# Retention values in products of 512 columns, second and last queries added behind their decayed keys, and the gated unit's operands loaded by halves

## The chip, the core and the metric

The kernel runs on one core of a Trainium2 chip. Its time is the device time of one execution in microseconds (us); where several runs are shown, the median counts. The profile is one execution of its own, whose instructions were recorded.

## What is computed

A trunk of two layers on an input x of 1024 tokens by 1024 channels, all in float32. Cut to what matters here:

```python
h = rmsnorm(x, norm_g[0])
u_s5, g_s5, q, k, v, g_ret = split(h @ w_in)          # 1024 x 1024 each, q and k 1024 x 512
# branch A: a diagonal complex state-space layer, then a gated linear unit
y = gelu(s5(u_s5));  y_s5 = y * sigmoid(y @ glu_w + glu_b) * silu(g_s5)
# branch B: retention, 8 heads, keys of 64 and values of 128, chunks of 64 tokens
q, k = rope(q) / 8, rope(k)                            # rotary positions
scores = q @ k.T * intra_decay                         # inside a chunk
kv = (k * k_decay).T @ v;  s = chunk_decay * s + kv    # state from chunk to chunk
y_ret = headnorm(scores @ v + (q * q_decay) @ s) * silu(g_ret)
x = x + concat(y_s5, y_ret) @ w_out
# layer 1: a gated causal convolution of 31 taps with its own normalisation, then a final rmsnorm
```

The output must agree with float32, so each projection is done as three products of rounded halves: `wh*xh + wh*xl + wl*xh`, where `h` is the rounded high part (type fp32r) and `l` is what is left.

## The kernel before

All activations lie transposed: 128 channels on the partitions, tokens along the free dimension, in two halves of 512 tokens. One tensor engine (PE) does the products; its instruction stream is written in program order and rearranged by a scheduler that looks at expected times, and every engine then works through its own list in order. So does SP, which issues nearly all DMAs: an issue that waits holds up all issues behind it.

**Weights.** `plan` writes down the order in which 512 KB weight blocks are used, `wnext` takes the next one and issues the loads of the two behind it, and `wload` loads a block (tile `wf`, three buffers), copies the high part on ACT (`wh`, line 133, three buffers) and subtracts for the low part on POOL (`wl`, line 134, three buffers). So the high part of a block can be made only once PE is through with the block three places before it, and its load only once POOL is through with that one.

**Retention** (`retention`, line 784 on) goes over four pairs of heads. For a pair, `ret_proj` projects keys and queries (`mm_k`, `mm_q`: 48 products of 512 columns each, the weights stationary), turns them by their positions, and then projects the values. Turning (`turn`) needs a copy of the raw tile with swapped 32-row blocks (`swp`, one buffer, four DMAs on SP, line 831), four products with the tables on POOL (lines 834 and 835) and two additions on DVE (line 836). The values (`mm_v`, lines 859 to 861) have the tokens as the stationary operand, and 256 columns of weights (one pair of heads) as the moving one: per pair 8 blocks of 128 tokens, each 24 products of 256 columns, collected in the three banks of `ps_mm` and scaled by ACT (line 862).

`ret_heads` then transposes the keys (`ktp`), multiplies them by the decay on DVE (`kt`, line 876), and does the small products `kv`, `sp`, `ro` and `rt`, with DVE work between them (states `S`, masked scores `sc`, normalisation). The scheduler puts the projections of the next pair between them, and after the last pair the products of the gated unit (`mm_glu`). I call this stretch, from the first `ktp` to the last `rt`, a **seam**.

`y_pass` reads the state-space result (`yp`), applies gelu on ACT (`yn`, line 781) and stores it; two of the eight go with each pair, and from the second pair on they wait for the last root of the pair before.

**The gated unit.** `load_split(self.yn_d, "y", False)` loads the eight operand blocks of 128 channels with all 1024 tokens each (`yf`, line 997, in the buffers of `wf`), and splits each half on ACT (`yh`, line 968) and DVE (`yl`, line 969). The split tiles take the place of the layer's first operands (`xh`, `xl`, still read by `mm_v`): those of the first half are free when the fourth token block of the last pair's values is done, those of the second when the eighth is.

The table of convolution taps (`convw`) is halved on DVE in line 1102 after its DMA. In `h1` the eight blocks `x1n` of the first half share five buffers with other tiles.

Of the kernel before, what the change touches and what calls it, by code (L numbers as in the profile page):

```python
# [11 lines left out]
F32 = mybir.dt.float32  # L12
# [27 lines left out]
class Trunk:  # L40
# [734 lines left out]
    def y_pass(self, rp, cb):  # L775

        nc = self.nc
        yt = rp.tile([P, 8, P], F32, name=f"yp_{cb}", tag="yp", bufs=1)
        nc.sync.dma_start(yt[:], self.y_d[cb].rearrange("i h g m -> (h g) i m"))
        yn = rp.tile([P, P, 8], F32, name=f"yn_{cb}", tag="ynt", bufs=2)  # L780
        nc.scalar.activation(yn[:], yt[:].rearrange("p i m -> p m i"), AF.Gelu_apprx_tanh)
        nc.sync.dma_start(self.yn_d[cb * P:(cb + 1) * P], yn[:].rearrange("p m i -> p (m i)"))

    def retention(self, st):
# [10 lines left out]
        self.g128 = rp.tile([P, 4], F32, name="g128")  # L795
        nc.sync.dma_start(self.g128[:], A["ret_g128"])
        for pair in range(4):
            cur = self.ret_proj(pair)
            with ExitStack() as held:
                if pair:  # L800
                    held.enter_context(self.tc.issue_after(self.last_rs.ins))
                for cb in (2 * pair, 2 * pair + 1):
                    self.y_pass(rq, cb)
            if pair == 3:
                early.close()
                self.lp = self.pool("l1", side="right")
            self.ret_heads(pair, *cur)

    def ret_proj(self, pair):
# [40 lines left out]
        vt = rp.tile([P, 8, 256], F32, name=f"v_{pair}", tag="v", bufs=2)  # L850
        for b in range(8):
# [10 lines left out]
            nc.scalar.mul(vt[:, b, :], ps[:, :256], self.Rtok[:, b:b + 1])  # L862
        return krot, qrot, vt

    def ret_heads(self, pair, K, Q, V):
        nc, rp = self.nc, self.rp
# [3 lines left out]
        for hf in range(2):  # L870
            ps = self.bank(f"ktp{hf}_{pair}")
            for b in range(4):
                t0 = (4 * hf + b) * P
                nc.tensor.transpose(ps[:, b * P:(b + 1) * P], K[:, t0:t0 + P], self.ident[:])
            kd = self.kdec[:, 2 * pair:2 * pair + 2, :].rearrange("p h d -> p (h d)")
            v.tensor_tensor(kt[:, 4 * hf:4 * hf + 4, :], ps[:].rearrange("p (b d) -> p b d", b=4),
                            kd.unsqueeze(1).broadcast_to([P, 4, P]), op=ALU.mult)

        S = rp.tile([P, 8, P], F32, name=f"S_{pair}", tag="S", bufs=1)
        for hf in range(2):  # L880
            ps = self.bank(f"kv{hf}_{pair}")
            for b4 in range(4):
# [3 lines left out]
                for hh in range(2):  # L886
                    r = slice(64 * hh, 64 * hh + 64)
                    nc.tensor.matmul(ps[r, b4 * P:(b4 + 1) * P], kt[:, b, r], V[:, b, hh * P:(hh + 1) * P],
                                     start=True, stop=True)
# [31 lines left out]
        for hf in range(2):  # L921
            pss = [self.bank(f"ro{hf}_{2 * pair + hh}") for hh in range(2)]

            def products():
# [7 lines left out]
                for hh in range(2):  # L932
                    for b4 in range(4):
                        b = 4 * hf + b4
                        yield nc.tensor.matmul(pss[hh][:, b4 * P:(b4 + 1) * P], sc[hh][:, b, :],
                                               V[:, b, hh * P:(hh + 1) * P], start=False, stop=b4 == 3)
            last_ro = self.chained(products())
# [28 lines left out]

    def split(self, src, hi, lo, eng):
        self.nc.scalar.copy(hi[:], src)  # L968
        eng.tensor_tensor(lo[:], src, hi[:].bitcast(F32), op=ALU.subtract)  # L969

    def layer0_back_and_layer1(self, st):
# [9 lines left out]
        def load_split(src, name, halves):  # L981
            res = [[], []]

            def put(kb, h, f):
                a, b = (self.op_tile(self.opA, f"A{h}", f"{name}{q}{kb}_{h}") for q in "hl")
                self.split(f, a, b, v)
                res[h].append((a, b))
            if halves:
                for h in range(2):
                    for kb in range(KB):  # L990
                        f = lp.tile([P, HALF], F32, name=f"{name}f{kb}_{h}", tag="tp", bufs=3)
                        nc.sync.dma_start(f[:], src[rows(kb), hs(h)])
                        put(kb, h, f[:])
            else:
                for kb in range(KB):
                    f = self.wp.tile([P, T], F32, name=f"{name}f{kb}", tag="wf", bufs=3)
                    nc.sync.dma_start(f[:], src[rows(kb)])
                    for h in range(2):
                        put(kb, h, f[:, hs(h)])
            return res  # L1000
# [8 lines left out]
        for nb, h in [(nb, h) for nb in range(6) for h in range(2)] + [(6, 0), (7, 0), (6, 1), (7, 1)]:  # L1009
# [13 lines left out]
            nc.scalar.mul(a[:], sg[:], 0.5)  # L1023
            v.scalar_tensor_tensor(b[:], sg[:], 0.5, a[:].bitcast(F32), op0=ALU.mult, op1=ALU.subtract)
            ys[h][nb] = (a, b)
# [22 lines left out]
        def h1(h):  # L1048
# [3 lines left out]
            for kb in range(KB):  # L1052
                t = (opB.tile([P, HALF], F32, name=f"x1n{kb}_{h}", tag="B1") if h else
                     lp.tile([P, HALF], F32, name=f"x1n{kb}_{h}", tag="u", bufs=5))
                nc.sync.dma_start(t[:], self.x1_d[rows(kb), hs(h)])
# [45 lines left out]
        nc.sync.dma_start(cw[:], A["conv_w"])  # L1101
        v.tensor_scalar(cw[:], cw[:], 0.5, None, op0=ALU.mult)
        cv = [[None] * 8 for _ in range(2)]
# [274 lines left out]
def layout(inp):  # L1378
# [61 lines left out]
```

## Time and profile before

| | |
|---|---|
| median of 3 runs | 1219.36 us (1218.27 to 1221.7) |
| the profiled execution, its own time | 1219.24 us |
| its span, from first to last instruction | 1217.5 us |
| granted clock of PE over the span | 0.997 |
| PE busy, DVE, POOL, ACT | 1199.5, 747.1, 653.9, 480.6 us |

What the execution takes outside the span is 1219.24 - 1217.5 = 1.7 us. In the rows of the profile, a group of instructions stands with its source line, engine and operation, what it writes and reads by tile name, the shapes, the count behind an x, and its busy time and mean duration. A row of the windows view gives the length of a stretch and, for each engine, its busy time and in brackets how many instructions touched it. In the timeline, square brackets give the idle time before an instruction and what ended it.

### The profile page before, as it was taken

Reading aid. Unit: us, or ns where it says so; the run is one execution under the profiler, and the core shown is the slowest. Engines: PE = TensorE matmul, PEld = TensorE weight load, DVE = VectorE, ACT = ScalarE, POOL = GpSimd, SP = SyncE. Lnnn points to the kernel's source line nnn. Section 1 sums busy time; section 2 is a strip of 40 time slices with the busy share of each in tenths; the row PEclk is TensorE's granted clock in tenths of the full one; section 3 lists DMA queues with packets and bytes.
Section 4 is the critical chain, followed back from the end, with each engine's and each line's share of the span. In section 5 each row is a group of like instructions: output and inputs, shape, how many; then the busy total and the mean of one; then the engine's idle time right before and its main releaser. Section 6 shows DMA issues by size and latency. Waiting matters only on the chain.

```text
span 1217.5 us, 17581 instructions
## 1 busy us (share of the span) xinstructions
PE 1199.5 (99%) x6660; PEld 1011.3 (83%) x6660; DVE 747.1 (61%) x1337; ACT 480.6 (39%) x712; POOL 653.9 (54%) x453
## 2 busy tenths in 40 slices
PE   9999999999999999998999999999999999999997
PEld 7888888888889999997888888788888888888876
DVE  7965555555413635546746101599999799999533
ACT  7212233322222323134434322545545575434652
POOL 2059988888124333342454551578453467758642
PEclk9999999999999999999999999999999999999998
DMA  8342433333384536266446776755677654356764
GB/s 333 104 139 74 152 128 124 133 131 124 107 268 139 176 102 195 82 216 220 165 156 216 269 270 254 260 188 196 222 253 251 232 182 155 123 176 236 243 250 147
DMA packets 98500, 225.03 MB, mean 185 GB/s; under 512 B 9072, under 2 KB 38000, under 8 KB 97776
## 3 DMA queue, kind: packets, MB, share of 16 engines
q1 hardware_dynamic: 98416, 223.92, 54.9%
q8 instruction: 52, 0.85, 0.3%
q14 instruction: 32, 0.26, 0.1%
HBM read 158.41 MB, written 61.28 MB: 180 GB/s over the span
## 4 chain that ended last, share of the span: by engine, by line
PE 91%; DMA 4%; DVE 2%; ACT 1%; POOL 1%; issue 1%; SPq 1%; DVEq 0%; POOLq 0%
PE mm_g L143 7%; PE mm_g L144 7%; PE mm_g L142 7%; PE mm_wo L144 5%; PE mm_wo L142 5%; PE mm_wo L143 5%; PE mm_a L144 2%; PE mm_b L144 2%; PE mm_a L143 2%; PE mm_a L142 2%; PE mm_b L143 2%; PE mm_u L144 2%; PE mm_u L143 2%; PE mm_b L142 2%; PE mm_u L142 2%; PE mm_glu L144 2%
## 5 line engine op out<-in xcount | busy, mean ns | idle before, releaser
L1142 DVE SCALAR_TENSOR_TENSOR cv<-u,convw,cv 128x512 f32<-128x512 f32 x398 | 273.4, 751 | 11.9 <-ACT cv L1128 9.6
L1122 POOL TENSOR_TENSOR tp<-tp,tp 128x512 f32<-128x512 f32 x64 | 83.1, 1298 | 44.4 <-ACT tp L1121 43.3
L144 PE MATMUL mm_g<-xh,wl_g 128*128 128x512 f32 x256 | 100.8, 394 | 0.0
L143 PE MATMUL mm_g<-xl,wh_g 128*128 128x512 f32 x256 | 100.6, 393 | 0.0
L142 PE MATMUL mm_g<-xh,wh_g 128*128 128x512 f32 x256 | 100.5, 393 | 0.0
L861 PE MATMUL mm_v<-wh_v,xl 128*128 128x256 f32 x256 | 72.5, 283 | 0.0
L860 PE MATMUL mm_v<-wl_v,xh 128*128 128x256 f32 x256 | 72.4, 283 | 0.0
L859 PE MATMUL mm_v<-wh_v,xh 128*128 128x256 f32 x256 | 72.4, 283 | 0.0
L134 POOL TENSOR_TENSOR wl_v<-wf_v,wh_v 128x1024 fp32r<-128x1024 f32 x8 | 19.2, 2396 | 88.6 <-ACT wh_v L133 88.6
L1121 ACT ACTIVATE tp<-u,convw 128x512 f32<-128x512 f32 x64 | 45.7, 719 | 34.9 <-POOL tp L1122 33.2
L325 DVE TENSOR_TENSOR gt<-mm_g,R 128x512 f32<-128x512 f32 x32 | 21.9, 685 | 59.9 <-PE mm_g L144 59.9
L143 PEld LDWEIGHTS mm_g<-xl,wh_g 128*128 128x128 f32 x256 | 48.1, 188 | 11.3 <-issue 1.6
L144 PEld LDWEIGHTS mm_g<-xh,wl_g 128*128 128x128 f32 x256 | 48.0, 188 | 10.6
L142 PEld LDWEIGHTS mm_g<-xh,wh_g 128*128 128x128 f32 x256 | 48.1, 188 | 9.6
L144 PE MATMUL mm_oc<-zh,wl_woc 128*128 128x512 f32 (+1 forms) x152 | 54.0, 359 | 1.5 <-DMA wl_woc<-lo_woc 1.5
L1044 DVE TENSOR_TENSOR x<-mm_wo,xr 128x512 f32<-128x512 f32 x16 | 11.1, 692 | 71.9 <-PE mm_wo L144 51.4
L142 PE MATMUL mm_oc<-zh,wh_woc 128*128 128x512 f32 (+1 forms) x152 | 54.3, 363 | 0.0
L143 PE MATMUL mm_oc<-zl,wh_woc 128*128 128x512 f32 (+1 forms) x152 | 53.8, 357 | 0.5 <-POOL zl L969 0.5
L143 PE MATMUL mm_glu<-yl,wh_glu 128*128 128x512 f32 x128 | 50.3, 393 | 2.5 <-DVE yl L969 2.5
L144 PE MATMUL mm_wo<-yrh,wl_wor 128*128 128x512 f32 x128 | 50.0, 391 | 1.4 <-DMA wl_wor<-lo_wor 1.4
L143 PE MATMUL mm_u<-xl,wh_u 128*128 128x512 f32 x128 | 50.1, 391 | 0.8 <-DVE xl L257 0.7
L142 PE MATMUL mm_glu<-yh,wh_glu 128*128 128x512 f32 x128 | 50.1, 393 | 0.6 <-ACT yh L968 0.6
(393 smaller groups left out, 3600.7 us busy)
## 6 DMA issues: line engine op xcount, KB each, us to landing
wf_g<-w_ab SPq DMA_DIRECT2D x16, 512.0 KB, 4.0
wf_wos<-w_out SPq DMA_DIRECT2D x16, 512.0 KB, 5.0
wf_wor<-w_out SPq DMA_DIRECT2D x16, 512.0 KB, 5.8
wf_cb<-w_c SPq DMA_DIRECT2D x16, 512.0 KB, 4.4
wf_ca<-w_c SPq DMA_DIRECT2D x16, 512.0 KB, 4.7
wf_woc<-w_out_c SPq DMA_DIRECT2D x16, 512.0 KB, 5.0
wf_cg<-w_c SPq DMA_DIRECT2D x11, 512.0 KB, 4.4
u_d<-ut SPq DMA_DIRECT2D x8, 512.0 KB, 3.2
```

Source lines behind the costliest of these rows:

```text
L134: lo[i].tensor_tensor(wl[:].rearrange(fl)[:, c], wf[:, c], h.bitcast(F32), op=ALU.subtract)
L142: nc.tensor.matmul(ps, wh[:, kb, :], xh, start=start, stop=False)
L143: nc.tensor.matmul(ps, wh[:, kb, :], xl, start=False, stop=False)
L144: self.last_mm = nc.tensor.matmul(ps, wl[:, kb, :], xh, start=False, stop=stop)
L325: nc.vector.tensor_tensor(gt[:, c], ps[:], self.R[:, c], op=ALU.mult)
L859: nc.tensor.matmul(ps[:, :256], xh[:, o:o + P], wh, start=kb == 0, stop=False)
L860: nc.tensor.matmul(ps[:, :256], xh[:, o:o + P], wl, start=False, stop=False)
L861: nc.tensor.matmul(ps[:, :256], xl[:, o:o + P], wh, start=False, stop=kb == KB - 1)
L1044: v.tensor_tensor(t[:], ps[:], xt[:], op=ALU.add)
L1121: nc.scalar.mul(sk[:], u[:, k:k + HALF], cw[:, nb, k:k + 1])
L1122: gp.tensor_tensor(s0[:], s0[:], sk[:], op=ALU.add)
L1142: v.scalar_tensor_tensor(dst[:], *tap, accs_[i][:], op0=ALU.mult, op1=ALU.add)
```

## The change

- **Values of pairs 0 and 1** are projected together, in place of pair 0's: 512 columns of weights (four heads) are the moving operand. The tokens go in two halves; for each half four banks of `ps_aux` (five are there) collect four token blocks at once, and the weights stream past them in four blocks. So each half loads and splits all four blocks: eight loads where two times two were before. Pair 1 then has no values of its own, and the keys of pair 2 are projected before its heads.
- **Queries of pairs 1 and 3** are added (line 836) behind the decayed keys `kt` of their own pair instead of before their values, and the swapped copy has two buffers.
- **The gated unit's operands** come by halves: eight loads of 128x512 for the first half of the tokens, two to a `wf` buffer, then eight for the second. The DVE splits of the second half are put behind the last `kt`.
- Smaller: `yn` in `y_pass` has one buffer instead of two; the taps are halved behind the gated unit; the last three `x1n` of the first half have buffers of their own; the pool of layer 1 is opened behind the last `kt`.

```diff
 def plan:
         for p in range(4):
             seq += [(A["w_ab"][28 + p], f"k{p}"), (A["w_ab"][24 + p], f"q{p}")]
-            seq += [(A["w_v"][2 * p + i], f"v{p}_{i}") for i in range(2)]
+            if p == 0:
+                seq += [(A["w_v"][j], f"v{p}_{h}_{j}") for h in range(2) for j in range(4)]
+            elif p > 1:
+                seq += [(A["w_v"][2 * p + i], f"v{p}_{i}") for i in range(2)]
 def y_pass:
-        yn = rp.tile([P, P, 8], F32, name=f"yn_{cb}", tag="ynt", bufs=2)
+        yn = rp.tile([P, P, 8], F32, name=f"yn_{cb}", tag="ynt", bufs=1)
 def retention:
+        ahead = None
         for pair in range(4):
-            cur = self.ret_proj(pair)
+            cur = list(ahead or self.ret_proj(pair))[-1]
+            ahead = pair == 1 and self.ret_proj(pair + 1)
+            if ahead:
+                next(ahead)
+            if pair == 0:
+                V = self.ret_values_wide()
+            elif pair > 1:
+                V = self.ret_values(pair)
...
 def ret_proj:
-            swp = self.rq.tile([P, T], F32, name=f"{nm}swp_{pair}", tag="swp", bufs=1)
+            swp = self.rq.tile([P, T], F32, name=f"{nm}swp_{pair}", tag="swp", bufs=2)
...
         project("k")
+        yield None
         krot, adds = turn("k")
         last = project("q")
         with self.tc.issue_after(last.ins):
             for add in adds:
                 add()
-        qrot, adds = turn("q")
-        for add in adds:
-            add()
+        qrot, qadds = turn("q")
+        if pair % 2 == 0:
+            for add in qadds:
+                add()
+            qadds = ()
+        yield krot, qrot, qadds
...
+    def ret_values_wide(self):
+        nc = self.nc
+        res = []
+        for h in range(2):
+            vt = self.rp.tile([P, 4, HALF], F32, name=f"v_0_{h}", tag="v", bufs=2)
+            pss = [self.bank(f"mm_v0_{h}_{b}") for b in range(4)]
+            for j in range(4):
+                wh, wl = (t[:].rearrange("p (k a) n -> p k (a n)", a=4) for t in self.wnext(f"v0_{h}_{j}"))
+                for b in range(4):
+                    o = slice(b * P, (b + 1) * P)
+                    for k in range(2):
+                        kb = 2 * j + k
+                        xh, xl = self.xs[h][kb]
+                        nc.tensor.matmul(pss[b][:], xh[:, o], wh[:, k, :], start=kb == 0, stop=False)
+                        nc.tensor.matmul(pss[b][:], xh[:, o], wl[:, k, :], start=False, stop=False)
+                        nc.tensor.matmul(pss[b][:], xl[:, o], wh[:, k, :], start=False, stop=kb == KB - 1)
+            for b in range(4):
+                nc.scalar.mul(vt[:, b, :], pss[b][:], self.Rtok[:, 4 * h + b:4 * h + b + 1])
+            res.append(vt)
+        return lambda p, b, hh: res[b // 4][:, b % 4, (2 * p + hh) * P:(2 * p + hh + 1) * P]
 def ret_heads:
+        with self.tc.issue_after(self.last_kt.ins):
+            for add in qadds:
+                add()
+        turned()
 def split:
+        with self.tc.issue_after(behind.ins) if behind else nullcontext():
-        eng.tensor_tensor(lo[:], src, hi[:].bitcast(F32), op=ALU.subtract)
+            eng.tensor_tensor(lo[:], src, hi[:].bitcast(F32), op=ALU.subtract)
 def load_split:
-                self.split(f, a, b, v)
+                self.split(f, a, b, v, None if halves or h == 0 else self.last_kt)
...
-                for kb in range(KB):
-                    f = self.wp.tile([P, T], F32, name=f"{name}f{kb}", tag="wf", bufs=3)
-                    nc.sync.dma_start(f[:], src[rows(kb)])
-                    for h in range(2):
-                        put(kb, h, f[:, hs(h)])
+                        if kb % 2 == 0:
+                            f2 = self.wp.tile([P, 2, HALF], F32, name=f"{name}f{kb}_{h}", tag="wf", bufs=3)
+                        f = f2[:, kb % 2, :]
+                        nc.sync.dma_start(f, src[rows(kb), hs(h)])
+                    put(kb, h, f)
 def h1:
-                     lp.tile([P, HALF], F32, name=f"x1n{kb}_{h}", tag="u", bufs=5))
+                     lp.tile([P, HALF], F32, name=f"x1n{kb}_{h}", **({"tag": "u", "bufs": 5} if kb < 5 else
+                                                                     {"tag": "tp", "bufs": 3})))
 taps:
-        v.tensor_scalar(cw[:], cw[:], 0.5, None, op0=ALU.mult)
+        with self.tc.issue_after(glu_end.ins):
+            v.tensor_scalar(cw[:], cw[:], 0.5, None, op0=ALU.mult)
 layout:
+    A["w_v"][:4] = w[:, 3072:3584].reshape(4, 2, P, HALF).transpose(0, 2, 1, 3).reshape(4, P, KB, P)
```

More of the change, by code (lines that the diff above doesn't have):

```diff
@@ L1 @@
 import math
-from contextlib import ExitStack, contextmanager
+from contextlib import ExitStack, nullcontext, contextmanager
 from itertools import chain
@@ L803, in retention, with turned @@
                     self.y_pass(rq, cb)
[L804 to L807, printed above, removed]
+            def turned():
+                if pair == 3:
+                    early.close()
+                    self.lp = self.pool("l1", side="right")
+            self.ret_heads(pair, *cur, V, turned)
     def ret_proj(self, pair):
@@ L844, in ret_proj, with ret_values @@
                 add()
-        qrot, adds = turn("q")
-        for add in adds:
-            add()
+        qrot, qadds = turn("q")
[4 more added lines that the diff above has]
+        yield krot, qrot, qadds
+    def ret_values(self, pair):
+        nc = self.nc
         wv = [self.wnext(f"v{pair}_{i}") for i in range(2)]
-        vt = rp.tile([P, 8, 256], F32, name=f"v_{pair}", tag="v", bufs=2)
+        vt = self.rp.tile([P, 8, 256], F32, name=f"v_{pair}", tag="v", bufs=2)
         for b in range(8):
@@ L862, in ret_proj, with ret_heads @@
             nc.scalar.mul(vt[:, b, :], ps[:, :256], self.Rtok[:, b:b + 1])
-        return krot, qrot, vt
-    def ret_heads(self, pair, K, Q, V):
+        return lambda p, b, hh: vt[:, b, hh * P:(hh + 1) * P]
+    def ret_values_wide(self):
+        nc = self.nc
+        res = []
[16 more added lines that the diff above has]
+        return lambda p, b, hh: res[b // 4][:, b % 4, (2 * p + hh) * P:(2 * p + hh + 1) * P]
+    def ret_heads(self, pair, K, Q, qadds, V, turned):
         nc, rp = self.nc, self.rp
@@ L935, in products @@
                         yield nc.tensor.matmul(pss[hh][:, b4 * P:(b4 + 1) * P], sc[hh][:, b, :],
-                                               V[:, b, hh * P:(hh + 1) * P], start=False, stop=b4 == 3)
+                                               V(pair, b, hh), start=False, stop=b4 == 3)
             last_ro = self.chained(products())
@@ L985, in put @@
                 a, b = (self.op_tile(self.opA, f"A{h}", f"{name}{q}{kb}_{h}") for q in "hl")
-                self.split(f, a, b, v)
+                self.split(f, a, b, v, None if halves or h == 0 else self.last_kt)
                 res[h].append((a, b))
-            if halves:
-                for h in range(2):
-                    for kb in range(KB):
[L991 to L994, printed above, removed]
-                for kb in range(KB):
-                    f = self.wp.tile([P, T], F32, name=f"{name}f{kb}", tag="wf", bufs=3)
-                    nc.sync.dma_start(f[:], src[rows(kb)])
-                    for h in range(2):
-                        put(kb, h, f[:, hs(h)])
+            for h in range(2):
+                for kb in range(KB):
+                    if halves:
+                        f = lp.tile([P, HALF], F32, name=f"{name}f{kb}_{h}", tag="tp", bufs=3)[:]
+                        nc.sync.dma_start(f, src[rows(kb), hs(h)])
+                    else:
+                        if kb % 2 == 0:
+                            f2 = self.wp.tile([P, 2, HALF], F32, name=f"{name}f{kb}_{h}", tag="wf", bufs=3)
+                        f = f2[:, kb % 2, :]
+                        nc.sync.dma_start(f, src[rows(kb), hs(h)])
+                    put(kb, h, f)
             return res
@@ L1023, in layer0_back_and_layer1 @@
             nc.scalar.mul(a[:], sg[:], 0.5)
[L1024 removed]
+            glu_end = v.scalar_tensor_tensor(b[:], sg[:], 0.5, a[:].bitcast(F32), op0=ALU.mult, op1=ALU.subtract)
             ys[h][nb] = (a, b)
```

8 lines of the change are left out of this document (4 added, 4 removed).

## The prediction

> **What bounds the kernel now.** I read the page's engine table first, then its groups, then the windows view over the stretches that the change touches, then who waits for whom there.
>
> ```profile
> span 1217.5 us, 17581 instructions
> PE 1199.5 (99%) x6660; PEld 1011.3 (83%) x6660; DVE 747.1 (61%) x1337; ACT 480.6 (39%) x712; POOL 653.9 (54%) x453
> L144 PE MATMUL mm_g<-xh,wl_g 128*128 128x512 f32 x256 | 100.8, 394 | 0.0
> L859 PE MATMUL mm_v<-wh_v,xh 128*128 128x256 f32 x256 | 72.4, 283 | 0.0
> ```
>
> PE is busy for 99% of the span, so the time changes where PE gets less work or waits less, and hardly anywhere else. The two group rows invite a mistake: 283 ns for a product of 256 columns and 394 ns for one of 512 look like a gain of 172 ns for each pair that is joined. But products overlap, so their durations can't be added. What one costs is the distance to the next start, a stretch divided by its count:
>
> ```profile
> 358.96:381.99 23.03, 23.03 (x192) 22.98 (x191) 3.21 (x7) 1.00 0.51 146
> 416.61:439.64 23.03, 23.03 (x192) 22.98 (x191) 3.33 (x7) 1.00 0.64 188
> ...
> 348.08:358.96 10.88, 10.88 (x48) 8.82 (x47) 0.69 (x1) 1.00 1.04 291
> 440.44:445.44 5.00, 5.00 (x21) 3.84 (x21) 0.00 (x0) 1.00 0.47 140
> ```
>
> The first two rows are the values of pairs 0 and 1, the third is `mm_q` of pair 0 (512 columns), the fourth a run of `mm_k` between small products. So 256 columns cost 23.03/192 = 0.120 us and 512 columns 10.88/48 = 0.2267 us, at a granted clock of 1.00. Joining two products of 256 saves 0.240 - 0.2267 = 0.013 us.
>
> The second place is the seam, the stretch from the first `ktp` to the last `rt` of a pair. Pairs 1, 2 and 3:
>
> ```profile
> 439.64:470.72 31.08, 31.08 (x228) 26.45 (x226) 19.38 (x71) 8.95 (x11) 7.10 (x3) 1.00 0.34 100
> 497.30:528.37 31.07, 31.07 (x227) 26.45 (x226) 19.38 (x71) 8.76 (x11) 7.09 (x3) 1.00 0.34 102
> 554.95:591.82 36.87, 33.26 (x229) 26.79 (x228) 27.87 (x86) 17.63 (x26) 9.38 (x5) 1.00 0.58 196
> ...
> PE mm_glu L143 <- DVE yl L969: 2.5, 3, 1.8
> PE mm_glu L142 <- ACT yh L968: 0.6, 1, 0.6
> ...
> 558.43 0.29 DVE L1102 TENSOR_SCALAR convw<-convw 128x248 f32<-128x248 f32 x1 [6.18 <-DMA convw<-conv_w]
> 558.64 1.29 DVE L969 TENSOR_TENSOR yl<-yf,yh 128x512 fp32r<-128x512 f32 x2
> ```
>
> The third seam has the same small products, and 83 large ones before its last `rt` instead of 81 (the program's list), yet it takes 5.79 us longer. PE stands idle for 36.87 - 33.26 = 3.61 us of it, waiting for split operands, and it hops between three accumulations. DVE itself sits 6.18 us on the DMA of the taps, with the operand splits queued behind.
>
> **The change, part by part.**
>
> *Values of pairs 0 and 1.* Removed: 2 x 192 products of 256 columns, 2 x 23.03 = 46.06 us. Added: 2 halves x 4 weight blocks x 24 = 192 products of 512 columns, 192 x 0.2267 = 43.53 us. On PE's path: -2.53 us. In the program's list a single large product now stands between the two key transposes of pair 0, one alternation more; the run of 21 shows what alternating costs, 5.00 - 21 x 0.2267 = 0.24 us. I take +0.24.
>
> [...]
>
> *The feed of the wide values.* The weights stream twice, so four more loads, four casts on ACT and four subtractions on POOL. A wide block lasts 24 x 0.2267 = 5.44 us; until now two blocks lasted 23.03 us. Here a new wait can arise, because POOL works through its list in order and the products for turning stand in it:
>
> ```profile
> 360.52 1.29 POOL L834 TENSOR_TENSOR kraw<-kraw,ropek 128x512 f32<-128x512 f32 x1 [8.91 <-DMA kswp<-kraw]
> 364.28 1.75 POOL L835 TENSOR_TENSOR kswp<-kswp,ropek 128x512 f32<-128x512 f32 x1
> 366.00 2.40 POOL L134 TENSOR_TENSOR wl_k<-wf_k,wh_k 128x1024 fp32r<-128x1024 f32 x1
> 374.22 1.29 POOL L834 TENSOR_TENSOR qraw<-qraw,ropeq 128x512 f32<-128x512 f32 x1 [5.82 <-DMA qswp<-qraw]
> ...
> 377.96 1.74 POOL L835 TENSOR_TENSOR qswp<-qswp,ropeq 128x512 f32<-128x512 f32 x1
> ...
> 359.16 0.69 DVE L822 TENSOR_TENSOR qraw<-mm_q,R 128x512 f32<-128x512 f32 x1 [4.75 <-PE mm_q L144]
> ...
> 358.97 1.05 ACT L133 CAST wh_k<-wf_k 128x1024 fp32r<-128x1024 f32 x1 [4.08 <-DMA kswp<-kraw]
> 364.43 2.09 ACT L781 ACTIVATE yn<-yp 128x1024 f32<-128x1024 f32 x1 [4.41 <-DMA yp<-y_d]
> ...
> 354.92 0.33 SPq L782 DMA_DIRECT2D yn_d<-yn  x1
> ...
> L831 SPq DMA_DIRECT2D qswp<-qraw x4: 517/590/1221, 369.0 to 371.4; - x4
> DMA to landing us min/median/max: 2.3/2.6/3.0
> ...
> wf_v<-w_v SPq DMA_DIRECT2D x8, 512.0 KB, 5.4
> ```
>
> The wide values begin where the values begin now, 358.96. Their third block takes the place of `wk` of pair 1 in these lists: cast at 358.97, low part at 366.00 to 368.40; PE wants it at 358.96 + 2 x 5.44 = 369.84, 1.4 us later. The swapped queries go out earlier: with two buffers the four DMAs need only the raw queries (359.16 + 0.69 = 359.85), not the turned keys; four issues of 0.59 and 3.0 to land give 365.2. POOL reaches them at 368.40, needs 379.70 - 374.22 = 5.48 us, and comes to the fourth block at 373.88. That block's cast waits for PE's first block (364.40) and ACT's gelu (366.52), so it is there. Low part ready: 373.88 + 2.40 = 376.28. PE arrives at 375.28, and its list puts four products with the high part first, 0.91 us. It waits 0.1 us; with the handover I take 0.2. Bounds: 0, and 4.5, priced below. The fifth low part is ready at 378.7, wanted near 381. The sixth block's load may start at 368.40 (its buffer), lands 5.4 later, and its cast waits for PE's third block, 375.3; low part 381.1, wanted at 386.4. From there POOL gains 3 us a block. The four banks of the second half come free one by one while the fifth serves. The single `yn` buffer makes the second gelu (364.43) wait for a store that was issued at 354.92: nothing.
>
> *Pair 1 without values.* Its `ktp` now comes 48 products of `mm_k` (10.88 us) behind its last `mm_q`, not 23.03.
>
> ```profile
> 418.47 1.75 POOL L835 TENSOR_TENSOR kswp<-kswp,ropek 128x512 f32<-128x512 f32 x1
> ...
> qswp<-qraw SPq DMA_DIRECT2D x16, 128.0 KB, 4.8
> ```
>
> POOL ends the turning of pair 1's keys at 420.22, 3.6 us after the last `mm_q` (416.61, where the values begin now), so the keys are there. The queries, added behind `kt`, are wanted about 17 us after it: 10.88, then 22 products of 0.2267, and the small ones. They come at 0.9 for the raw tile, 2.4 for four issues, 4.8 to land and 5.48 on POOL, 13.6, and some more where SP waits for a store. Covered by 3 us: 0, at worst +2.
>
> *The third seam.* With the second half's splits behind `kt` and the taps out of DVE's way, it can run as the other two: 5.79 less the two extra products (0.45) is 5.34 us. What replaces the wait is a chain of reloads, since two pairs of `yf` must be split before their buffers take the next:
>
> ```profile
> L969 DVE TENSOR_TENSOR yl<-yf,yh x16: 680/684/1782, 548.2 to 574.0; 128x512 fp32r<-128x512 f32 x16
> ...
> L968 ACT CAST yh<-yf x16: 609/617/625, 541.1 to 572.8; 128x512 fp32r<-128x512 f32 x16
> ...
> yf<-yn_d SPq DMA_DIRECT2D x8, 512.0 KB, 3.5
> wf_glu<-w_glu SPq DMA_DIRECT2D x8, 512.0 KB, 4.0
> ```
>
> The values of pair 3 start 23.03 us before that seam. Their first operands come free in the fourth token block, 9.0 us in. First pair at the slow end of DVE's rows: 9.0 + 0.62 + 2 x 1.78 = 13.2; reload 3.5; third pair split by 16.7 + 0.62 + 2 x 0.68 = 18.7, fourth by about 20.5. All of it is inside 23.03, with 2.5 us to spare. For the second half DVE is fuller: the 8 splits (5.5 us) come on top of its 19.38 in a 31 us seam, and the later scores stand behind the first gate, which stands behind a weight load of 4.0. I take a residue of 0.4 us, the neighbouring row being the 0.6 that `mm_glu` waited for ACT, between 0 and the 3.61 that are idle now. Term: -5.34 + 0.4 = -4.94 us.
>
> *The loads of `x1n`.*
>
> ```profile
> PE mm_wo L144 <- DMA wl_wor<-lo_wor: 1.4, 1, 1.4
> ...
> 759.11 3.09 SPq L1055 DMA_DIRECT2D x1n<-x_d  x3
> 763.16 0.32 SPq L119 DMA_DIRECT2D wl_wor<-lo_wor  x1
> ```
>
> Three loads stood ahead of the one that PE then waits for; they move ahead. But that load also waits for PE to release its buffer, so I count 0, with -1.4 as the other end.
>
> **Sum**, against the profiled execution's 1219.24 (median 1219.36, 0.1 away): -2.53 + 0.24 + 0.2 - 4.94 = -7.0, so 1212.2 us.
>
> **Rivals.**
>
> *The seam stays* (0.10). The chain of reloads overruns by more than its 2.5 us, and PE waits for operands as now: 1219.24 - 2.53 + 0.24 + 0.2 = 1217.2. For it: four loads in series, each behind ACT and DVE. Against it: the arithmetic above, with slow rows.
>
> *The turned queries hold up the feed* (0.05).
>
> ```profile
> L831 SPq DMA_DIRECT2D kswp<-kraw x8: 582/591/997, 349.0 to 410.0; - x8
> DMA to landing us min/median/max: 4.5/7.2/10.4
> ```
>
> If the swapped queries took the 10.4 us of the slowest swapped keys, POOL would begin them at 362.2 + 10.4 = 372.6, the fourth low part would be ready 5.48 + 2.40 later, at 380.5, and PE would lose 380.5 - 376.2 = 4.3 us plus 0.2 for the handover, 4.5 in place of 0.2: 1216.5. Against it: those keys competed with megabytes of tables (a DMA share of 1.04 in the row 348.08:358.96).
>
> *Slower: the feed paces the wide values* (0.05). If SP, held by another issue, lets no load go before its turn, each of the five blocks that reuse a buffer takes load, cast and split in series, 5.4 + 1.05 + 2.40 = 8.85 us instead of 5.44: 5 x 3.41 = 17.1, so 1229.3. It turns into a loss that a measurement can tell from 2.1 us a block. For it: the new loads stand behind the gelu stores in SP's list. Against it: the gelu row at 364.43 ends before any of these loads could start for want of a buffer (368.40).
>
> *The wide product is worth more than the starts say* (0.02). By the durations in the rows the values would gain 384 x 0.283 - 192 x 0.394 = 33.0 us, giving about 1182. [...]
>
> **The numbers.** The forecast, 1212.2, has 0.78, and its own bounds run from 1210 (no residue, the `x1n` wait gone) to 1215. With the first two rivals the range is 1209.8 to 1217.2. A measurement of this kernel can tell about 0.3% from no change, 3.7 us, so 1215.6 and 1222.9 are the edges: faster 0.80 (the forecast and the last rival), same 0.15, slower 0.05.
>
> **What would show it.** Right: a stretch of 192 `mm_v` products of 512 columns in 43.5 to 44.5 us; a third seam near 31.5; no wait of PE for `wl_v` over 0.5. Wrong: PE waiting for `wl_v` on POOL, or for `yl` or `yh` as now; a `ktp` of pair 1 or 2 that waits for `krot`; distances between 512 column products other than 0.2267.

## The result and the profile after

The changed kernel takes 1213.18 us (median of 6 runs, 1211.89 to 1214.82); the kernel before, run beside it, 1219.26. The ratio is 0.9949, interval 0.9937 to 0.9960: 6.1 us less, where 7.0 had been forecast (1212.2). On a second chip, in the comparison `r1_after` below, the ratio was 0.9969 (0.9959 to 0.9979).

The profiled execution took 1212.99 us, its span is 6.3 us shorter than before. The head of its page, which answers to the first rows of the prediction:

```profile
span 1211.2 us, 17238 instructions
PE 1195.8 (99%) x6468; PEld 1001.7 (83%) x6468; DVE 748.2 (62%) x1337; ACT 479.9 (40%) x706; POOL 664.0 (55%) x457
```

There are 192 products fewer, and PE is still busy for 99%. The windows view of the changed kernel, over the wide values, the seam of pair 0, the third seam, and the third seam with the gated unit up to its end (the first output product):

```profile
359.26:402.78 43.52, 43.52 (x193) 35.99 (x192) 9.98 (x5) 15.20 (x16) 30.33 (x16) 1.00 0.52 159
402.78:434.03 31.25, 31.25 (x227) 26.61 (x226) 19.59 (x71) 9.23 (x11) 4.80 (x2) 1.00 0.28 82
...
552.53:586.37 33.84, 32.03 (x228) 27.04 (x227) 28.11 (x81) 13.57 (x21) 13.55 (x7) 1.00 0.65 230
...
552.53:655.00 102.47, 100.66 (x531) 83.80 (x529) 63.82 (x117) 41.97 (x65) 45.16 (x25) 1.00 0.56 195
```

And of the kernel before, for the seam of pair 0, the third seam by the same marks, and the third seam with the gated unit:

```profile
381.99:413.27 31.28, 31.28 (x228) 26.66 (x227) 19.58 (x71) 9.11 (x11) 7.10 (x3) 1.00 0.37 112
...
554.95:592.02 37.07, 33.46 (x230) 26.99 (x229) 28.07 (x86) 17.63 (x26) 9.58 (x5) 1.00 0.58 196
...
554.95:660.20 105.25, 101.64 (x531) 83.39 (x530) 65.85 (x122) 45.47 (x69) 41.91 (x23) 1.00 0.55 187
```

The wide values run without a pause, 43.52 us for 192 products. From the first value to the last pair's first `ktp` the kernel before takes 554.95 - 358.96 = 195.99 us, the changed one 552.53 - 359.26 = 193.27: 2.72 less. From there to the end of the gated unit, where both do the same products, 105.25 - 102.47 = 2.78 less. The third seam alone is shorter by 3.23 us, but it holds two large products fewer (0.45 us), which come later. What PE waits for in the changed kernel, the longest:

```profile
PE ro L979 <- DVE sc L959: 1.7, 1, 1.7
...
PE mm_a L148 <- DMA wl_ca<-lo_ca: 1.1, 1, 1.1
```

The waits for `yl` and `yh` are gone, and so is the one for `wl_wor`. A new one stands first: in the third seam PE waits for the masked scores. DVE's timeline there:

```profile
561.53 1.57 DVE L947 SCALAR_TENSOR_TENSOR S<-S,g,kv 128x128 f32<-128x128 f32 x4
564.86 0.69 DVE L1019 TENSOR_TENSOR yl<-yf,yh 128x512 fp32r<-128x512 f32 x1 [1.76 <-ACT yh L1017]
565.46 0.34 DVE L947 SCALAR_TENSOR_TENSOR S<-S,g,kv 128x128 f32<-128x128 f32 x1
565.72 1.28 DVE L959 TENSOR_TENSOR sc<-sp,retmask 128x512 f32<-128x512 f32 x2
```

DVE stands 1.76 us at the seventh split of the second half, whose load came late, and the scores are behind it in the list, though the first products they need were done at 561.4.

### The profile page after: what moved, and what is told of

It reads as the page before. It is cut to its first block, busy times and chain, and to the rows that moved or that the text cites. A ratio compares the mean times of both kernels' runs of the same rounds, so it can differ in the third digit from the quotient of the medians.

```text
span 1211.2 us, 17238 instructions
## 1 busy us (share of the span) xinstructions
PE 1195.8 (99%) x6468; PEld 1001.7 (83%) x6468; DVE 748.2 (62%) x1337; ACT 479.9 (40%) x706; POOL 664.0 (55%) x457
## 4 chain that ended last, share of the span: by engine, by line
PE 94%; DMA 2%; ACT 2%; DVE 1%; issue 0%; SPq 0%; POOL 0%; DVEq 0%
PE mm_g L148 7%; PE mm_g L147 7%; PE mm_g L146 7%; PE mm_wo L148 5%; PE mm_wo L146 5%; PE mm_wo L147 5%; PE mm_a L148 2%; PE mm_b L147 2%; PE mm_b L148 2%; PE mm_a L146 2%; PE mm_a L147 2%; PE mm_b L146 2%; PE mm_u L148 2%; PE mm_u L147 2%; PE mm_u L146 2%; PE mm_glu L146 2%
## 5 line engine op out<-in xcount | busy, mean ns | idle before, releaser
L138 POOL TENSOR_TENSOR wl_v<-wf_v,wh_v 128x1024 fp32r<-128x1024 f32 x12 | 29.0, 2425 | 51.9 <-ACT wh_v L137 51.9
L1066 POOL TENSOR_TENSOR yg<-yg,yn 128x512 f32<-128x512 f32 x16 | 22.5, 1404 | 53.5 <-DMA yg<-gs_d 15.6
L148 PE MATMUL mm_a<-h1h,wl_ca 128*128 128x512 f32 x128 | 50.3, 393 | 1.1 <-DMA wl_ca<-lo_ca 1.1
L146 PE MATMUL mm_g<-h1h,wh_cg 128*128 128x512 f32 x128 | 50.4, 394 | 0.0
L146 PE MATMUL mm_b<-h1h,wh_cb 128*128 128x512 f32 x128 | 50.2, 392 | 0.0
L146 PE MATMUL mm_wo<-yrh,wh_wor 128*128 128x512 f32 x128 | 50.2, 392 | 0.0
```

The lines of the kernel that those rows point to most:

```text
L138: lo[i].tensor_tensor(wl[:].rearrange(fl)[:, c], wf[:, c], h.bitcast(F32), op=ALU.subtract)
L146: nc.tensor.matmul(ps, wh[:, kb, :], xh, start=start, stop=False)
L148: self.last_mm = nc.tensor.matmul(ps, wl[:, kb, :], xh, start=False, stop=stop)
L1066: gp.tensor_tensor(yg[:], yg[:], yn[:], op=ALU.mult)
```

## The experiments

Each group shared one chip and its runs of the kernel before. The chips differ (before: 1220.83, 1218.69 and 1221.96 us), so ratios are compared inside a group, and mechanisms by stretches of the traces. The ratios are those on record, with their intervals; a ratio of the two medians can differ from them by 0.2%. Where a saving in us stands beside a ratio, it is worked out from it. Where `r1_after` is not named, the stretches are set against the first traces of the kernel before and of the changed kernel, taken on another chip; each is one execution.

### Each part alone, and the columns

**e1_cols256**: the changed kernel, each wide product as two of 256 columns.

```diff
-nc.tensor.matmul(pss[b][:], xh[:, o], wh[:, k, :], ...)
+for c in (slice(i, i + 256) for i in range(0, HALF, 256)):
+    nc.tensor.matmul(pss[b][:, c], xh[:, o], wh[:, k, c], ...)
```

> The changed kernel with one edit: each wide value product of 512 columns is done as two of 256 into the two halves of its bank; weights, banks, order and all else stay. Theory (fixed cost of about 13 ns for each product, whatever its width): the stretch of the wide values goes from 43.52 us to 384 x 0.120 = 46.1, so the time rises by 2.5 us, to 1215.7. [...] Rival (the gain of the values lies in the order and the feed, not in the width): no change, 1213.2.

Measured: 1221.09, ratio 0.9979 (0.9959 to 0.9999). The stretch of the wide values, and the wait in it:

```profile
359.19:406.47 47.28, 46.33 (x386) 46.12 (x385) 9.97 (x5) 15.06 (x16) 30.91 (x16) 1.00 0.55 163
```

```profile
PE mm_v L903 <- POOL wl_v L138: 0.9, 1, 0.9
```

Without the idle 0.95 us it is 46.33 us, 2.8 more than with 512 columns; the median start to start is 0.120 us. So the width brings the gain of the values, as the theory said. The total also holds waits further on (1.2 us for pair 1's queries, 91.61 us in place of 87.15 for the first half of the output projection), and the changed kernel was not run on this chip, so the two totals cannot be set against each other.

**e3_wide_only**: the kernel before with the wide values alone (with `ahead`, two `swp` buffers and pair 1's queries behind its keys). The edit is that part of the diff above.

> The kernel before with the first part alone: wide values of pairs 0 and 1, with the keys of pair 2 ahead and pair 1's queries behind its decayed keys; the gated unit's operands, the taps, the x1n buffers and pair 3's queries stay as before. Theory (the parts add up, and the values bring 2.5 to 2.7 us up to the third seam): third seam near 37 us as before, PE idle there near 3.6, time 1219.3 - 2.7 = 1216.6, and 1.4 less if the later wait for wl_wor goes for a reason other than x1n. Rival (the earlier order also eases the third seam): third seam 34, time near 1213.5.

Measured: 1219.13, ratio 0.9983 (0.9969 to 0.9996), 2.1 us less. Two stretches, the wide values and the third seam with the gated unit, and two waits:

```profile
359.63:403.40 43.77, 43.77 (x194) 35.91 (x192) 9.98 (x5) 15.14 (x16) 30.82 (x16) 1.00 0.57 169
...
554.17:660.57 106.40, 103.18 (x531) 84.92 (x529) 64.92 (x122) 46.00 (x70) 42.90 (x23) 0.98 0.56 182
```

```profile
PE mm_glu L147 <- DVE yl L1019: 1.2, 3, 0.5
...
PE sp L953 <- DVE qrot L851: 0.8, 1, 0.8
```

The third seam and the gated unit cost what they cost before and 1.15 more, so the wide values alone do not ease the seam, as the theory had it. The second wait was not in the changed kernel's first profile: pair 1's turned queries come too late for their scores.

**e4_seam_only**: the kernel before with the operands by halves, the second half's splits behind the keys, and the taps behind the gated unit.

> The kernel before with the seam's part alone: the gated unit's operands by halves with the second half's splits behind the decayed keys, and the taps halved behind the gated unit. Theory (the parts add up): third seam 37.07 to about 33.8 us, time 1219.3 - 3.2 = 1216.1, with the wait of 1.4 for wl_wor still there. Rival (the gain of the seam hangs on pair 3's queries being put behind its keys, or on the order of the wide part): third seam above 36, time 1218 to 1219.

Measured: 1223.80, ratio 1.0013 (0.9999 to 1.0027): no gain. The values of pair 3, and what PE waited for in them:

```profile
532.20:561.57 29.37, 24.79 (x193) 24.59 (x192) 13.99 (x13) 8.62 (x16) 13.84 (x10) 0.94 0.63 204
```

```profile
PE mm_v L859 <- ACT v L862: 4.6, 1, 4.6
```

The third seam with the gated unit:

```profile
561.57:662.04 100.47, 100.24 (x530) 83.57 (x529) 56.99 (x113) 42.20 (x62) 39.91 (x23) 1.00 0.57 184
```

The rival was right that there is no gain, though not with its number: the seam's wait is gone (by the halves or by the taps, which this kernel cannot tell apart), and a worse one stands ahead of it. The two operands that need a reload are cast on ACT before the scaling of the values; their reload waits for DVE's splits, which stand behind the queries; PE finds no free bank for 4.6 us.

**e9_all_scores_first**: the changed kernel, with the last two splits of the second half and the first gate behind the last `sc`.

```diff
-self.split(f, a, b, v, None if halves or h == 0 else self.last_kt)
+self.split(f, a, b, v, None if halves or h == 0 else self.last_kt if kb < 6 else self.last_sc)
```

> The changed kernel with DVE's list rearranged in the third seam: the splits of the last two operand blocks of the second half, and the first gate, are put behind all four masked scores (sc). Theory (DVE stands 1.76 us at a split whose load is late, the scores wait behind it, and PE waits 1.7 to 1.9 us for the first score): the wait of ro for sc goes, third seam 33.84 to about 31.8, time 1211.2. Rival (the late operand is the bound, whatever stands before it): mm_glu waits for yl or yh instead by 1 to 2 us, time 1213.

Measured: 1220.05, ratio 0.9988 (0.9971 to 1.0006). The third seam with the gated unit:

```profile
553.62:653.94 100.32, 100.15 (x530) 83.29 (x529) 62.67 (x114) 39.31 (x59) 41.17 (x23) 1.00 0.56 187
```

The wait for the scores is gone, and this stretch is 2.15 us shorter than in the changed kernel (102.47). Yet the total is not. PE's waits, and the windows view in steps of 2 us behind the gated unit (the third figure from the end is the granted clock):

```profile
PE mm_wo L146 <- ACT wh_wor L137: 2.1, 1, 2.1
PE mm_wo L148 <- POOL wl_wos L138: 1.7, 1, 1.7
```

```profile
672.00:674.00 2.00, 1.05 (x5) 0.55 (x3) 0.00 (x0) 0.51 (x1) 0.00 (x0) 1.00 0.99 337
674.00:676.00 2.00, 0.73 (x2) 0.30 (x2) 1.29 (x2) 2.00 (x4) 0.87 (x1) 1.00 0.60 236
676.00:678.00 2.00, 1.18 (x3) 0.73 (x4) 0.00 (x0) 1.47 (x3) 2.00 (x2) 0.66 0.70 251
678.00:680.00 2.00, 2.00 (x6) 1.52 (x6) 0.00 (x0) 0.00 (x0) 2.00 (x2) 0.50 0.60 159
680.00:682.00 2.00, 2.00 (x7) 1.52 (x5) 0.00 (x0) 0.00 (x0) 2.00 (x1) 0.50 0.85 309
682.00:684.00 2.00, 2.00 (x7) 1.62 (x6) 0.00 (x0) 0.00 (x0) 0.17 (x1) 0.64 0.77 285
684.00:686.00 2.00, 2.00 (x10) 1.65 (x10) 0.37 (x1) 0.47 (x1) 0.00 (x0) 1.00 1.02 410
```

PE comes to the first output products and waits for their weights, and then its clock drops to 0.50. By these rows the loss by the clock is about 2 x (0.34 + 0.50 + 0.50 + 0.36) = 3.4 us, on top of 3.8 us for the two waits shown. The first half of the output projection takes 96.09 us in all, 8.94 more than in the changed kernel. Neither theory had this: the seam's part of mine was right and its sum wrong. Why the weights come late here, no run isolates.

### The parts of the seam, on another chip

**r1_after**: the changed kernel itself.

> The changed kernel itself, unedited, for a comparison on the chip of the next three. Theory (the gain is made on TensorE's path and does not hang on how fast transfers land): 0.995 of the kernel before, as in the first result. Rival (the feed of the output projection behind the gated unit, where two edited versions lost 2 to 6 us to waits of mm_wo for wl_wos, is worse in this program wherever transfers land late): 0.997 to 1.000, with mm_wo waiting 2 to 6 us for low parts.

Measured: 1214.16 (1212.39 to 1217.10), ratio 0.9969 (0.9959 to 0.9979), 3.8 us less; 0.995 lies outside. The rival's mechanism was not seen either: in this profile the first half of the output projection takes 741.13 - 653.63 = 87.50 us, against 87.13 before. The next stretch is its third seam with the gated unit:

```profile
551.94:653.63 101.69, 100.66 (x530) 83.81 (x529) 62.71 (x117) 41.11 (x64) 44.85 (x25) 1.00 0.56 194
```

It is 3.56 us shorter than before. Its profiled execution took 1212.67 us, near the fast end; what the longer ones wait for is open. A hint is the profile of e7_x1n_u below, which differs only in `x1n` and is a long one: there pair 1's queries come 1.5 us late, and the first half of the output projection takes 90.89 us.

**e10_q3_early**: the changed kernel, pair 3's queries added before its values (`if pair != 1:` in place of `if pair % 2 == 0:`).

> The changed kernel with pair 3's queries added before its values again, as in the kernel before; all else stays. Theory (the halves need the queries out of DVE's way: DVE stands at the add until the swapped queries land, the splits behind it free the reload buffers late, ACT stands at the late operand with the scaling of the values behind it, and PE waits for a free bank): mm_v of pair 3 waits 3 to 5 us for ACT, time 2 to 4 us over the changed kernel. Rival (it is the order of the loads alone): no wait of mm_v, time within 1 us of the changed kernel.

Measured: 1217.24, ratio 0.9991 (0.9981 to 1.0002): 3.1 us over `r1_after` by the medians. But `mm_v` did not wait. The wait came in the seam:

```profile
PE sp L953 <- DVE S L947: 3.2, 1, 3.2
```

```profile
552.86:657.41 104.55, 101.33 (x530) 84.71 (x529) 58.66 (x118) 45.97 (x70) 41.95 (x24) 0.98 0.56 190
```

So the price was as the theory said and the place was not: the late splits now stood ahead of the states `S` in DVE's list. Halves need the late queries, here as in e4_seam_only; whole blocks do not (e13 below).

**e5b_no_halves**: the changed kernel with whole operand blocks as before, their splits not put behind `kt`.

> The changed kernel with the gated unit's operands in whole blocks again, as in the kernel before, and their splits not put behind the decayed keys; queries, taps, wide values and x1n stay changed. Theory (the halves bring the seam's gain): third seam 36 to 37 us, mm_glu waits for yl and yh by 2 to 3 us, time 3 us over the changed kernel. Rival (the taps and the queries brought it): third seam 34, time within 1 us.

Measured: 1212.87, ratio 0.9962 (0.9947 to 0.9978). Third seam, and with the gated unit:

```profile
552.10:587.00 34.90, 34.72 (x241) 29.37 (x240) 29.46 (x85) 20.16 (x28) 12.70 (x7) 1.00 0.76 275
552.10:652.68 100.58, 100.40 (x530) 83.70 (x529) 64.19 (x120) 47.00 (x69) 42.57 (x24) 1.00 0.61 211
```

My theory fell: without the halves PE idles 0.18 us there, and the stretch is 1.1 us shorter than in `r1_after`, on the same chip. The seam's gain is not made by the halves. Whether they cost anything is not shown: behind the gated unit this kernel takes 741.90 - 652.68 = 89.22 us for the first half of the output projection, `r1_after` 87.50, so that by its end the 1.1 us are gone, and the intervals of the two times overlap.

**e7_x1n_u**: the changed kernel with all `x1n` of the first half in five buffers.

> The changed kernel with all eight x1n of the first half in the five shared buffers again. Theory (three loads that stood ahead of the last wl_wor load are gone from there, and with them the wait of 1.4 us): the wait of mm_wo for wl_wor is back with 1.0 to 1.5 us, time 1.4 over the changed kernel. Rival (the wait went because PE releases that buffer earlier, as the third seam and the glu end earlier): no wait, no difference.

Measured: 1214.32, ratio 0.9970, as `r1_after`; the wait did not come back, though the three loads stood ahead of `wl_wor` again. The load of `wl_wor`, before and in this kernel:

```profile
L119 SPq DMA_DIRECT2D wl_wor<-lo_wor x1: 320/320/320, 763.2 to 763.2; - x1
...
DMA to landing us min/median/max: 4.9/4.9/4.9
```

```profile
L123 SPq DMA_DIRECT2D wl_wor<-lo_wor x1: 319/319/319, 764.3 to 764.3; - x1
...
DMA to landing us min/median/max: 3.4/3.4/3.4
```

In both it goes out 5.83 us after the same product (`r_R`, 757.33 and 758.44), when PE releases its buffer, so the three loads did not hold it back; it lands 1.5 us sooner here. Why is open, and this one profile does not clear the edit: in the other three with the shared buffers (e3, e4, e11) the load landed after 4.6 to 4.7 us and PE waited 1.0 to 1.1, and in all eight profiles without them it landed after 3.2 to 3.4 and PE did not wait for it. The two times agree, but their intervals, some 1.2 us either way, could hide 1.4. The rival had the right outcome, but not the reason. The profiled execution here is the longest of its 12 (1218.43).

### Queries or taps

**e11_before_q3_taps**: the kernel before with two small edits.

```diff
-        qrot, adds = turn("q")
-        for add in adds:
-            add()
+        qrot, qadds = turn("q")
+        if pair != 3:
+            for add in qadds:
+                add()
+            qadds = ()
...
+        with self.tc.issue_after(last_kt.ins):
+            for add in qadds:
+                add()
+        turned()
...
+        with self.tc.issue_after(glu_end.ins):
             v.tensor_scalar(cw[:], cw[:], 0.5, None, op0=ALU.mult)
```

> The kernel before with two small edits alone: pair 3's queries added behind its decayed keys (and the last pool opened there), and the taps halved behind the gated unit. Values stay narrow and the gated unit's operands stay in whole blocks. Theory (what held the third seam up was DVE standing at the taps and at the queries, with the splits behind; the halves bring nothing, as the run without them showed): third seam 37.07 to about 34.9 with more gated products in it, from the last pair's first ktp to the end of the gated unit 105.0 to 100.5 us, time 3.5 to 4.5 us under the kernel before, 0.9967. Rival (the wide values' order is needed too): under 1.5 us.

Measured: 1218.96, ratio 0.9974 (0.9958 to 0.9990), 3.2 us less. The third seam with the gated unit, and DVE where it stood 6.18 us at `convw` before:

```profile
555.53:655.81 100.28, 100.28 (x530) 83.68 (x529) 64.89 (x119) 46.36 (x68) 41.91 (x24) 1.00 0.63 211
```

```profile
553.87 1.29 DVE L976 TENSOR_TENSOR yl<-yf,yh 128x512 fp32r<-128x512 f32 x2 [5.87 <-ACT yh L975]
556.17 1.29 DVE L878 TENSOR_TENSOR kt<-ktp,kdec 128x512 f32<-128x512 f32 x2 [1.01 <-PE ktp L876]
```

These two edits (with them the pool of layer 1 is opened behind `kt`, as in the changed kernel) bring 4.97 us from the third seam's start to the end of the gated unit, more than the whole change does there (2.78 and 3.56), and PE does not idle in it. The keys come 1.0 us after their transposes. In this profile more than that is lost behind it: the first half of the output projection takes 93.89 us (655.81 to 749.70), where before had 87.13. It is one of the longest of its 12 executions (1221.96).

**e12_whole_taps_early** and **e13_whole_q3_early**: the changed kernel with whole blocks, and one of the two edits undone in each.

> The changed kernel with whole operand blocks, and with the taps halved where they were in the code before; pair 3's queries stay behind its keys. Theory (the taps are what held DVE up): DVE stands at the taps for several us with splits behind it, PE waits 1 us or more, time 1.5 us over the same kernel with late taps (0.9962 of before there, so 0.9975). Rival (with the pool opened behind the keys the taps come late in DVE's list in any case, and the queries carry the gain): no difference, 0.996.

> The changed kernel with whole operand blocks, and with pair 3's queries added before its values; the taps stay late. Theory (the queries carry the gain): the splits stand behind the add that waits for the swapped copy, PE waits for yl and yh as in the kernel before, time 3 us over the version with late queries, 0.9985 of before. Rival (the taps carry it): no difference, 0.996.

Measured: 1218.33, ratio 0.9965 (0.9951 to 0.9980), and 1215.70, ratio 0.9942 (0.9924 to 0.9961). The third seam with the gated unit, e12 and e13:

```profile
556.55:657.25 100.70, 100.39 (x530) 83.69 (x529) 62.78 (x120) 46.22 (x68) 41.51 (x24) 1.00 0.63 208
```

```profile
557.01:657.65 100.64, 100.47 (x531) 83.69 (x529) 62.70 (x119) 44.66 (x67) 42.76 (x23) 1.00 0.58 190
```

Both rivals were right by these stretches; e12's time alone would also allow its theory. Either edit alone does it, since either takes `convw` from in front of `kt` in DVE's list: the taps lie where the queries' tiles lay, so with late queries their load goes out later (at 566.9 in e12, against 553.6 before), and the scheduler puts their halving behind the scores even where nothing orders it. With neither edit, in e3_wide_only, it stands in front as before. The pool is opened behind `kt` in all three, so that is not what differs:

```profile
555.53 1.10 DVE L1152 TENSOR_SCALAR convw<-convw 128x248 f32<-128x248 f32 x1 [5.12 <-DMA convw<-conv_w]
556.55 1.28 DVE L1019 TENSOR_TENSOR yl<-yf,yh 128x512 fp32r<-128x512 f32 x2
557.75 1.27 DVE L920 TENSOR_TENSOR kt<-ktp,kdec 128x512 f32<-128x512 f32 x2
```

In the kernel before, the keys stand behind `convw` and two splits in the same way, 3.9 us after the end of their transposes (555.99):

```profile
559.84 1.28 DVE L876 TENSOR_TENSOR kt<-ktp,kdec 128x512 f32<-128x512 f32 x2
```

What held the third seam up was one small instruction on `convw`, 0.29 us of work, that waited 6.18 us for its DMA with keys and splits queued behind it.

Both profiles show something else, ahead of the third seam. PE waits in pair 1's seam for the turned queries, 2.1 us in e12 and 1.9 in e13, where the clock then falls to 0.50:

```profile
PE sp L953 <- DVE qrot L851: 1.9, 1, 1.9
```

```profile
458.00:460.00 2.00, 0.17 (x1) 0.21 (x2) 1.96 (x3) 0.00 (x0) 1.13 (x1) 1.00 0.71 217
460.00:462.00 2.00, 2.00 (x9) 1.57 (x9) 1.44 (x5) 0.00 (x0) 0.00 (x0) 0.91 0.96 326
462.00:464.00 2.00, 2.00 (x11) 1.25 (x12) 2.00 (x5) 0.00 (x0) 0.00 (x0) 0.50 1.08 252
464.00:466.00 2.00, 2.00 (x23) 1.88 (x22) 1.40 (x3) 0.00 (x0) 0.10 (x1) 0.74 0.78 229
```

From the first value to the third seam these two take 197.21 and 197.58 us, longer than the kernel before (195.99): in such an execution the gain of the wide values is lost before the third seam begins. In e12 the DMAs for the swapped queries start 1.5 us later than in the changed kernel (443.6 against 442.1) and land later, and POOL begins the turning at 450.88 in place of 447.97.

**e2_cols128**: each wide product as four of 128 columns, as in e1.

> The changed kernel with each wide value product of 512 columns done as four of 128, everything else in place. Theory (a product costs its columns at 0.4167 ns plus a fixed 13 ns, as 0.120 us at 256 and 0.2267 at 512 say): 0.0667 us a product, 768 of them 51.2 us in place of 43.5. Rival (each product also loads its 128 stationary columns, and below some width that load no longer hides behind the product before): about 0.109 us a product, as for ktp and rt at 128 columns, 83.7 us.

```profile
359.68:445.38 85.70, 85.70 (x769) 85.70 (x768) 9.89 (x5) 15.13 (x16) 30.19 (x16) 1.00 0.32 96
```

The rival was right: 85.70/768 = 0.1116 us each, hardly less than at 256 columns, and the whole is 41 us above the kernel before on its chip (1263.07, one run).

## Why the prediction was right

Time, range and direction held; on the second chip the gain was 3.8 us by the ratio, little over half of the forecast. The total is also in part luck. Up to the end of the first half of the output projection the gain is 2.72 + 2.78 - 0.02 = 5.5 us in the profile, where the forecast had all of its 7.0; the other 0.8 us come from behind, where it had nothing. The sign that I had named, a third seam near 31.5, did not come: it took 33.84. Step by step, on the profiled executions:

- *Values*, -2.53 forecast: 46.06 to 43.52, -2.54. e1 shows that the width does it. The durations' -33 did not come. But my reason, a fixed cost of 13 ns on each product, was wrong: e2 would then have cost 0.067 us a product, and it took 0.1116. The rows speak for the load of the stationary operand as what sets the pace at 128 columns and nearly at 256: the weight loads are busy for all 85.70 us of e2's stretch and 46.12 of e1's 46.33, but for 35.99 of 43.52 at 512. No run changes the load alone.
- *Alternation*, +0.24: nothing (31.25 against 31.28). *Feed*, +0.2: nothing in this profile, 0.9 in e1; the place was right, the bound of 4.5 never came near.
- *Pair 1's queries*, 0, at worst +2: none in the changed kernel's two profiles nor in e5b. In the other kernels with this part the wait was there, 0.2 (e10) to 2.2 (e2), and behind the one of 1.9 (e13) the clock cost about 1.7 us more. So the cover of 3 us is spent in most of these profiles, and my worst case of +2 was too low, because it had no loss by the clock.
- *Third seam*, -4.94: measured -2.78 and -3.56 to the end of the gated unit. The term was mis-sized by its residue, taken as 0.4: the third seam stays 33.84 - 31.08 = 2.76 us above the second seam of the kernel before, 1.81 of it idle (the scores' wait of 1.7 above all) and 0.95 in which PE is busy longer for the same products. And it was credited to the wrong edit. I read the 6.18 us on `convw` rightly as what held DVE up, but let the halves share in the gain: the taps' place is worth 4.97 with the late queries (e11), and with whole blocks either of the two edits brings it (e12, e13) and the stretch is 1.1 shorter than with halves (e5b).
- *`x1n`*, 0 with -1.4 as the other end: the wait went, but not because the load went out earlier, which PE's release sets (5.83 us after `r_R` in both); it landed after 3.2 us in place of 4.9. Whether the edit did that is open (e7). That made up for some of the seam, by luck. Over half of it came back as the wait for `wl_ca`, 0.3 before, 1.1 now.
- *Rivals*: the seam staying was the nearest to a miss. e4 is that rival and worse: without late queries the chain of reloads overruns and stops the values. The order in which the queries come was thus the condition of the halves, and I had not named it.

## What to carry over

DVE's list was a queue here (in the kernel before it stood 6.18 us at `convw`, with splits and keys behind it): before a wait is given a remedy, look at the instruction that stands at its head, and move that. One small operation on late data ahead of the critical ones cost 5 us here, and one edit that moved it did as much up to the end of the gated unit as the rebuilding of the loads. A gain in one stage was not always kept in the next: in the profiles of e9 and e11 the time made up to the end of the gated unit (4.93 and 4.97 us against the kernel before) was lost again behind it (96.09 and 93.89 us in place of 87.13), where PE reached weights that were not ready and waited 2.1 and 1.9 us for `wh_wor`. That it was lost because PE came earlier is argued, not shown. And a cover of 3 us, worked out from one profile, did not hold in most of the others: see what a wait costs when the cover fails before counting it as nothing.

## What the hardware showed unexpectedly

- **A floor under a product's cost.** With its own load of 128 stationary columns, start to start was 0.2267 us at 512 moving columns, 0.120 at 256, 0.1116 at 128. In e2 the loads of the stationary operand were busy for all 85.70 us of the stretch.
- **A wait of 2 us cost nearly as much again.** In e13 the clock fell to 0.50 after the wait of 1.9 us; by the rows above that lost 2 x (0.09 + 0.50 + 0.26) = 1.7 us more. In e9 an idle stretch of 2.05 us (673.06 to 675.11, cut in two by the windows), with 0.22 and 0.76 us more by 677.57, went with 3.4 us lost. One wait of 1.7 us in the changed kernel's third seam, and one of 1.75 among the 3.61 us in pieces before, left it at 1.00 (the windows rows above). The idle time alone does not tell the cases apart: in e7_x1n_u 1.64 us of it in pieces (674 to 678) was followed by a clock of 0.50 (678 to 680), and in e12 2.17 us in pieces (674 to 680) left it at 1.00. What decides it, no run here shows.
